# RWKV-7 mixer in a two-layer trunk: v without its head mean in the states, gate products on Vector, joins of the inverse cut into parts between products of v

## The chip, the cores and the metric

The kernel runs on one core of a Trainium2 chip. The metric is the device time of one execution in microseconds (us), median of several runs. TensorE's clock has two levels, 1.2 and 2.4 GHz; the profile gives the granted one as a share of the full clock.

## What is computed

A trunk of two layers over 256 tokens of width 1024: each layer is a feed-forward, a mixer, a feed-forward and a gated embedding, with RMS norms around each. The mixer of the first layer is a gMLP, that of the second an RWKV-7 mixer with 16 heads of 64, and only the latter is touched. Cut to what matters:

```python
r, k, v = ...                                 # three products of 1024x1024
g = sigmoid(xg @ g1) @ g2                     # gate, 1024 -> 160 -> 1024
y = wkv7_scan(r, decay, k, v, -kk, kk * a)    # state 64x64 per head:
#   S = S diag(w) + (S a) b^T + v k^T ;  y = S r     (i: value, j: key)
mean = mean(y, -1); var = mean((y - mean) ** 2, -1)      # over a head's 64 values
yn = (y - mean) * rsqrt(var + eps) * lnx[0] + lnx[1]
bonus = sum(r * k * r_k, -1) * v              # one factor for each token and head
out = ((yn + bonus) * g) @ w_out
```

Each row of the state belongs to one value dimension, and rows never mix. So the mean of y over a head's value dimensions is the y that the mean of v would give.

## The kernel before, in words

The program is one straight line of eight stages. Weights come in units of 128 rows: a load of 512 KB on SyncE's queue (`raw`, L134), a rounded high part by Scalar (L154) and the remaining low part by Vector (L156), three TensorE products for each pair. A table `on_pool` gives the low part of five of the eight units of the output weights `o` (`bwout`) to Pool. The weights of r, k, v and of the second gate product g2 are used in full precision and come as 1 MB loads (`wf`, L146) straight into a slot.

There are 20 slots of 128x2048 and 8 PSUM banks, both handed out in order from queues of free ones, so a load may start when the use of whatever held its slot has ended. A scheduler fixes the order on each engine from the order of the text; `behind(...)` ties work to come after a named instruction.

The mixer works in 4 chunks of 64 tokens (two blocks b of 128 tokens, two chunks in each). Its stages, with the names in the rows:

- The products r (L1174, in PSUM `r`) stand after the preparation of decay and keys, and are moved by the scheduler around two `triangle(i)` (L1033, `m`): products of keys whose triangles are to be inverted. Vector inverts diagonal blocks of 16 by forward substitution (L1069, L1071), between the transposes L1061 and L1072, L1073.
- Gate: `gate1` (L1129, four transposes L1140), `gate2` for both blocks (L1150, L1153), with the result `gn`.
- v: eight steps k of four products 128x512 (L1238). From step 2 on each step is followed by an `inside(k)` (L1218 `sc`, L1226 `rb`: products within a chunk, masked by Vector in L1221, L1228), and from step 4 on by a `join(i)`: the blocks of 16 are joined to 32 (`q` L1081, then `x` L1088) and to 64 (`q` L1098, then `x` L1112), each with a copy or an addition by Scalar or Vector behind it. One join is 128 or 64 small matrix products.
- `stack_v`: Scalar writes v into the states' stack `sv` (L1267, L1268, eight times 64x512). `tb` and the copies `bn` (L1308) turn keys. `bonus`: Pool multiplies v by the bonus factor and adds `lnx[1]` (L1293, L1294).
- `chunk(c)`, four times, one after the other through the state: `us` (L1337), `y` (L1357), `us` (L1363), copies to `sv` (L1365 Scalar, L1366 Vector), `st` (L1375) and the update (L1380, Vector), `y` (L1387). Then the norm of y: head mean and subtraction (L1399, L1400, L1402, `gs` and `yc`, Vector), square by Scalar (L1416), its sum `gv` (L1417 Vector, L1418 and L1419 Pool), the product `yo` (L1429 Vector).
- `gains(b, q)`, behind chunks 0 and 1: Pool multiplies v's share by the gate (L1167) and the gate by `lnx[0]` (L1168).
- `tail`: `yo` by the gate plus v's share (L1435, L1436), transposes (L275), then the output product `Dn` (L178 to L180, `o`).

## Time and profile before

| | |
|---|---|
| median of 3 runs | 1206.67 us (1204.51 to 1207.19) |
| the profiled execution, by the clock | 1207.52 us |
| its span in the profile | 1205.7 us, 18609 instructions |
| TensorE busy | 1160.7 us (96%) |
| Vector busy | 839.7 us (70%) |
| Scalar busy | 650.0 us (54%) |
| Pool busy | 98.3 us (8%), 109 instructions |
| DMA | 207.78 MB, mean 172 GB/s |
| instruction blocks loaded (queue q8) | 57, 0.93 MB |

The profile page cuts the span into 40 slices. TensorE is busy for nine tenths or more in nearly all of them; the dip, together with one of the granted clock, is in slices 27 to 32, about 785 to 960 us, the RWKV mixer. Times below are from the start of the span; a row `L1174 MATMUL r<-xr,wf` is an instruction of line 1174 that writes tile `r` from `xr` and `wf`, `x48` that 48 such stand together (a product of full precision, as all of r, v, gate and joins are, is counted twice there, and once in the orders of the next section), and the bracket behind it the idle time ahead of the first and what ended it. `issue` is a wait for nothing that the profile shows. Engines: PE is TensorE, PEld its weight load, DVE Vector, ACT Scalar, POOL GpSimd, SP SyncE.

### The profile page before, as it was taken

What the parts mean: (1) busy time and instruction counts of PE and PEld (TensorE: products, weight loads), DVE (VectorE), ACT (ScalarE), POOL (GpSimd) and SP (SyncE); (2) the same over time, 40 slices, a digit from 0 to 9 for tenths busy, and PEclk for the clock granted to TensorE, in tenths of its full rate; (3) what the DMA queues carried; (4) which work ended last, traced back from release to release, by engine and by line L of the source; (5) the groups of instructions that cost most, each with busy time, mean ns of one, the idle gap of its engine ahead of it and who ended that gap; (6) DMA issues with size and microseconds to landing.
All of it is one profiled execution on the core that took longest, in us unless ns stands there. A gap on an engine that the chain in (4) does not pass through costs nothing. (4 is left out here: it accounts for less than half of the span.)

```text
span 1205.7 us, 18609 instructions
## 1 busy us (share of the span) xinstructions
PE 1160.7 (96%) x7252; PEld 954.4 (79%) x7252; DVE 839.7 (70%) x1272; ACT 650.0 (54%) x1125; POOL 98.3 (8%) x109
## 2 busy tenths in 40 slices
PE   8999999999999999999999999989987799999997
PEld 6888888888888888888888887576566678888886
DVE  5887667686787676668767644698355888766663
ACT  6665556454576555568655532454053276555553
POOL 0000001010010000012000001300009420000011
PEclk8999999999999999999999999998998799999999
DMA  7886655656667666655666573113103267666510
GB/s 249 299 282 194 193 174 165 238 163 204 211 207 242 184 188 192 181 171 183 233 196 193 185 275 132 33 48 140 37 3 106 71 204 268 207 183 194 172 57 36
DMA packets 58778, 207.78 MB, mean 172 GB/s; under 512 B 6721, under 2 KB 7233, under 8 KB 58433
## 3 DMA queue, kind: packets, MB, share of 16 engines
q1 hardware_dynamic: 58688, 206.59, 52.6%
q8 instruction: 57, 0.93, 0.3%
q14 instruction: 33, 0.26, 0.1%
HBM read 205.51 MB, written 1.05 MB: 171 GB/s over the span
## 5 line engine op out<-in xcount | busy, mean ns | idle before, releaser
L156 DVE TENSOR_TENSOR w<-raw,w 128x1024 fp32r<-128x1024 f32 x335 | 408.0, 1224 | 142.3 <-ACT w L154 136.2
L154 ACT CAST w<-raw 128x1024 fp32r<-128x1024 f32 x340 | 357.5, 1056 | 154.3 <-PE mm L400 65.3
L400 PE MATMUL mm<-xT,w 128*128 128x512 f32 (+1 forms) x2304 | 407.8, 337 | 0.0
L400 PEld LDWEIGHTS mm<-xT,w 128*128 128x128 f32 x2304 | 358.5, 189 | 50.0
L178 PE MATMUL acc<-w,hT 128*128 128x512 f32 x352 | 138.2, 393 | 0.0
L179 PE MATMUL acc<-w,hT 128*128 128x512 f32 x352 | 137.3, 390 | 0.0
L180 PE MATMUL acc<-w,hT 128*128 128x512 f32 x352 | 137.1, 389 | 0.0
L408 ACT COPY pn<-mm 128x256 f32<-128x256 f32 x144 | 46.6, 375 | 99.2 <-PE mm L400 99.2
L409 DVE TENSOR_TENSOR pn<-mm,pn 128x256 f32<-128x256 f32 x144 | 54.3, 419 | 47.4 <-ACT pn L408 47.4
L180 PEld LDWEIGHTS acc<-w,hT 128*128 128x128 f32 x352 | 66.1, 188 | 14.2
L178 PEld LDWEIGHTS acc<-w,hT 128*128 128x128 f32 x352 | 66.2, 188 | 12.6
L179 PEld LDWEIGHTS acc<-w,hT 128*128 128x128 f32 x352 | 66.3, 188 | 12.3
L232 POOL TENSOR_SCALAR rpost<-ss 128x1 f32<-128x1 f32 x15 | 7.4, 494 | 770.8 <-ACT junk L239 770.8
L178 PE MATMUL mm<-w,xT 128*128 128x512 f32 x128 | 51.8, 414 | 3.7 <-ACT w L154 3.1
L179 PE MATMUL mm<-w,xT 128*128 128x512 f32 x128 | 51.7, 407 | 0.6 <-DVE xT L289 0.5
L289 DVE SCALAR_TENSOR_TENSOR xT<-tr,gT,xT 128x128 fp32r<-128x128 f32 x112 | 35.7, 344 | 23.5 <-ACT xT L288 22.7
L412 DVE TENSOR_TENSOR pn<-pn,yc 128x512 f32<-128x512 f32 x72 | 49.7, 690 | 2.1
L180 PE MATMUL mm<-w,xT 128*128 128x512 f32 x128 | 50.9, 403 | 0.0
L179 PE MATMUL z<-w,xT 128*128 128x512 f32 x128 | 49.9, 390 | 0.0
L180 PE MATMUL z<-w,xT 128*128 128x512 f32 x128 | 49.9, 390 | 0.0
L178 PE MATMUL z<-w,xT 128*128 128x512 f32 x128 | 49.7, 393 | 0.0
L288 ACT ACTIVATE xT<-tr,gT 128x128 fp32r<-128x128 f32 x112 | 37.9, 372 | 19.3 <-PE tr L275 15.2
(277 smaller groups left out, 1546.9 us busy)
## 6 DMA issues: line engine op xcount, KB each, us to landing
raw<-in_w SPq DMA_DIRECT2D x264, 512.0 KB, 4.2
raw<-in_win SPq DMA_DIRECT2D x32, 512.0 KB, 4.3
wf<-in_wrkv SPq DMA_DIRECT2D x12, 1024.0 KB, 5.2
raw<-in_wout SPq DMA_DIRECT2D x16, 512.0 KB, 4.7
raw<-in_wg SPq DMA_DIRECT2D x16, 512.0 KB, 4.0
gbc<-in_norm_g SPq DMA_DIRECT2D x9, 512.0 KB, 4.7
...
```

What stands on the lines that cost most here:

```text
L154: self.high = self.nc.scalar.copy(hh, r[:p, :n])
L156: eng.tensor_tensor(ll, r[:p, :n], hh.bitcast(F32), op=ALU.subtract)
L178: mm(out, lhsT=lh, rhs=rh, start=start, stop=False)
L179: mm(out, lhsT=ll, rhs=rh, start=False, stop=False)
L180: mm(out, lhsT=lh, rhs=rl, start=False, stop=stop)
L232: nc.gpsimd.tensor_scalar(r, a, b, eps, op0=ALU.add, op1=ALU.add)
L288: done = (nc.scalar.activation(hi, v, AF.Copy, scale=gc), nc.vector.scalar_tensor_tensor(lo, v, gc, hi.bitcast(F32), op0=ALU.mult, op1=ALU ...
L289: nc.vector.scalar_tensor_tensor(lo, v, gc, hi.bitcast(F32), op0=ALU.mult, op1=ALU.subtract))
L400: nc.tensor.matmul(ps[i][:, :T] if s else ps[i], lhsT=w[:, sl], rhs=x, start=u + q + s == 0, stop=s + u == 2 and q == 3)
L408: nc.scalar.copy(zi, ps[i][:, T:])
L409: nc.vector.tensor_tensor(zi, ps[i][:, :T], zi, op=ALU.add)
L412: nc.vector.tensor_tensor(z2, z2, rbc.unsqueeze(1).to_broadcast([128, 2, T]), op=ALU.mult)
```

## The change

1. The table for Pool goes; all low parts of `o` are Vector's (L156).
2. The r products (`r_step(k)`) stand in the text by the triangles: steps 0 to 3 ahead of the first, 4 to 6 ahead of the second, 7 behind.
3. v starts right behind `gate1`; `gate2` comes behind v, among the parts of join 3. The gate's transposes are apart (`gate_t`), behind the first step of v. The mixing products for v (L822) stand ahead of Vector's transpose L1072. The load of g2 is issued ahead of the first of v, into the slot of `hnT`; v's first goes to that of `dxT`.
4. Every join is cut into four parts, which stand between the four products of a step of v (joins 0 to 2 in steps 5, 6, 7) or with `gate2` (join 3). The insides come later: 0 and 1 behind step 5, 2 and 3 behind step 6, 4 to 7 behind step 7.
5. `vm`, the head mean of v, is taken once (Vector), and `stack_v` puts v less its mean into the states (Vector, one operation for each 64x512). The mean of y is zero then, so the three Vector operations on it in each chunk become one Scalar copy `yc`. The bonus still uses all of v.
6. `gains()`: Vector forms, ahead of the chunks, the gate times `lnx[0]` (`gx`), times `lnx[1]` (`lg`) and times the bonus factor; `vgain(b)` behind chunks 0 and 1 takes v by the last and adds `lg`. Pool's L1293, L1294, L1167, L1168 go. Both `lnx` rows are loaded early, ahead of the last r weights.

```diff
-        share = (("o", (0, 2, 5, 6, 7)),)
-        self.on_pool.update(at[n] + k for n, ks in share for k in ks)
...
+        def r_step(k):
+
+            w = self.need(at["r"] + k // 2)[0][:, k % 2]
+            for m in range(KT):
+                mm(psr[m // 2][:, (m % 2) * T:(m % 2 + 1) * T], lhsT=w[:, m * 128:(m + 1) * 128], rhs=xent(0, k),
+                   start=k == 0 and m % 2 == 0, stop=k == KT - 1 and m % 2 == 1)
+            if k % 2:
+                self.release(at["r"] + k // 2)
+
         for i in range(2):
             if i:
                 squares(i)
             decay(i)
             V.tensor_tensor(bt[:, hs(i)], kk[:, hs(i)], av[:, hs(i)], op=ALU.mult)
             ab(i)
+            for k in (range(4, 7) if i else range(4)):
+                r_step(k)
             triangle(i)
+        r_step(7)
         self.drop(eo)
+        self.drop(X["x"][0])
...
+        def pieces(n, do, last):
+
+            r = [lambda lo=lo: do(range(lo, lo + n // 4)) for lo in range(0, n, n // 4)]
+            return r[:3] + [lambda: (r[3](), last())]
+
         def join(i):
...
+                def do(ns):
+                    for n in ns:
+                        for o in range(0, 128, 32):
+                            mm(ps[o:o + 32, n * 16:(n + 1) * 16], lhsT=nx[o:o + 16, n, :], rhs=wv[o:o + 16, n, 0:16], start=True, stop=True)
+
+                def last():
+                    S.copy(qn[:, :, 0:16], ps.rearrange("p (n t) -> p n t", t=16))
+                    self.unbank(ps)
...
+            return pieces(32, do, last)
...
+        def gate_t():
+
+            gl, ps = G8["s"], G8["p"]
+            gn = gl[:, 1024:1536].rearrange("p (b n) -> p b n", b=2)
...
+            return [lambda: main(0), lambda: main(1), rest]
...
+        def gains():
 
             gn = X["gn"]
-            if b == 0 and q == 0:
-                G8["la"] = self.gain_tile(io["lnx"][0:1, :])
-            bs = slice(b * D + q * 512, b * D + (q + 1) * 512)
-            G.tensor_tensor(vn[:, bs], vn[:, bs], gn[:, bs], op=ALU.mult)
-            G.tensor_tensor(gn[:, bs], gn[:, bs], G8["la"][:, q * 512:(q + 1) * 512], op=ALU.mult)
-
-
-        for k in range(KT):
-            w = self.need(at["r"] + k // 2)[0][:, k % 2]
+            X["gx"], X["lg"] = self.slot("gx"), self.slot("lg")
+            la, lb = (self.gain_tile(io["lnx"][n:n + 1, :]) for n in range(2))
+            for b in range(NB):
+                bs = slice(b * D, (b + 1) * D)
+                V.tensor_tensor(X["gx"][:, bs], gn[:, bs], la, op=ALU.mult)
+                V.tensor_tensor(X["lg"][:, bs], gn[:, bs], lb, op=ALU.mult)
+                g3 = gn[:, bs].rearrange("p (h t) -> p h t", t=64)
+                V.tensor_tensor(g3, g3, bon[:, b * 16:(b + 1) * 16].unsqueeze(2).to_broadcast([128, 16, 64]), op=ALU.mult)
...
+        def vgain(b):
+
+            for q in range(2):
+                bs = slice(b * D + q * 512, b * D + (q + 1) * 512)
+                V.tensor_tensor(vn[:, bs], vn[:, bs], X["gn"][:, bs], op=ALU.mult)
+                V.tensor_tensor(vn[:, bs], vn[:, bs], X["lg"][:, bs], op=ALU.add)
...
-        X["gn"] = self.slot("gn")
-        for b in range(NB):
-            gate2(b)
...
+        def v_step(k, between=()):
+
             x = xent(2, k)
             w = self.need(at["v"] + k // 2)[0][:, k % 2]
+            between = list(between)
             for b in range(NB):
                 for q in range(2):
                     mm(psv[b][q], lhsT=x[:, b * 128:(b + 1) * 128], rhs=w[:, q * 512:(q + 1) * 512], start=k == 0, stop=k == KT - 1)
+                    if between:
+                        between.pop(0)()
             if k % 2:
                 self.release(at["v"] + k // 2)
-            if k in (1, 3):
-                P(1, 0)
-            if k > 1:
-                inside(k - 2)
-            if k > 3:
-                if k == 7:
-                    self.drop(X["x"][2])
-                    xx = self.slot("xx")
-                    xv = xx.rearrange("p (n t) -> p n t", t=64)
-                    for o in (32, 96):
-                        G.memset(xv[o:o + 32, :, 0:32], 0.0)
-                join(k - 4)
-        inside(6)
-        inside(7)
+
+        v_step(0)
+        gate_t()
+        v_step(1)
+        P(1, 0)
+        v_step(2)
+        v_step(3)
+        P(1, 0)
+        v_step(4)
+        xx = self.slot("xx")
+        xv = xx.rearrange("p (n t) -> p n t", t=64)
+        for o in (32, 96):
+            G.memset(xv[o:o + 32, :, 0:32], 0.0)
+        v_step(5, join(0))
+        inside(0)
+        inside(1)
+        v_step(6, join(1))
+        self.drop(nq)
+        bo_sums()
+        P(2, 4)
+        inside(2)
+        inside(3)
+        v_step(7, join(2))
+        self.drop(X["x"][2])
+        X["gn"] = self.slot("gn")
+        inside(4)
         vn = self.slot("vn")
         for b in range(NB):
             for q in range(2):
                 S.copy(vn[:, b * D + q * 512:b * D + (q + 1) * 512], psv[b][q])
         self.unbank(*psv[0], *psv[1])
+        inside(5)
+        j3 = join(3)
+        g2 = gate2(0)
+        for n in range(2):
+            g2[n]()
+            j3[2 * n]()
+            j3[2 * n + 1]()
+        g2[2]()
+        self.drop(wu_, mx)
+        inside(6)
+        for n in gate2(1):
+            n()
+        inside(7)
+        gains()
...
+        vm = self.small(32, "vm", 1)
+        vmv = vm.rearrange("p (b m h) -> p b m h", b=2, h=2)
+        for b in range(NB):
+            V.tensor_reduce(vm[:, b * 16:(b + 1) * 16], vn[:, b * D:(b + 1) * D].rearrange("p (h t) -> p h t", t=64), axis=AX.X, op=ALU.add)
+            V.tensor_scalar(vm[:, b * 16:(b + 1) * 16], vm[:, b * 16:(b + 1) * 16], ck[:, 0:1], 1.0 / 64, op0=ALU.mult, op1=ALU.mult)
 
         def stack_v(c):
             rs = half[c % 2]
-            S.activation(svv[c // 2][OD, c % 2, :, 0, :], vv[rs, c // 2, :, 0, :], AF.Copy, scale=ck[rs, 0:1])
-            S.activation(svv[c // 2][EV, c % 2, :, 1, :], vv[rs, c // 2, :, 1, :], AF.Copy, scale=ck[rs, 0:1])
+            for h in range(2):
+                V.scalar_tensor_tensor(svv[c // 2][half[1 - h], c % 2, :, h, :], vv[rs, c // 2, :, h, :], ck[rs, 0:1],
+                                       vmv[rs, c // 2, :, h].unsqueeze(2).to_broadcast([64, 8, 64]), op0=ALU.mult, op1=ALU.subtract)
...
-                    s = self.small(4, "gs", 4)
-                    V.tensor_reduce(s, yv_, axis=AX.X, op=ALU.add)
-                    V.tensor_scalar(s, s, 1.0 / 64, None, op0=ALU.mult)
                     yc = self.small(256, "yc", 4)
-                    L["n"] = V.tensor_tensor(r4(yc), yv_, s.unsqueeze(2).to_broadcast([128, 4, 64]), op=ALU.subtract)
+                    L["n"] = S.copy(yc, yp[:, :256])
...
-                e.tensor_tensor(yo[:, sl], yo[:, sl], X["gn"][:, sl], op=ALU.mult)
+                e.tensor_tensor(yo[:, sl], yo[:, sl], X["gx"][:, sl], op=ALU.mult)
...
         chunk(0)
-        with behind("n"):
+        with behind("c"):
             P(1, 0)
-            for q in range(2):
-                gains(0, q)
+            vgain(0)
         chunk(1)
-        with behind("n"):
+        with behind("c"):
             P(1, 0)
-            for q in range(2):
-                gains(1, q)
+            vgain(1)
+        self.drop(X["gn"], X["lg"])
```

What moves on the engines, at three places. First TensorE at join 0 (`q`, 32x16 products of the inverse) and the step of v around it; `rb` is the end of an inside. Before:

```order
L1226 MATMUL rb_7290<-sk_7197,bt_6873 64x64 x8
L1081 MATMUL q_596_7311<-wu_6759,nq_6996 32x16 x128
L1238 MATMUL v_7218<-wf_7263,xr_7177 128x512
L1238 MATMUL v_7219<-wf_7263,xr_7177 128x512
L1238 MATMUL v_7220<-wf_7263,xr_7177 128x512
L1238 MATMUL v_7221<-wf_7263,xr_7177 128x512
```

And now:

```order
L1296 MATMUL v_7194<-wf_7225,xr_7153 128x512
L1099 MATMUL q_584_7234<-wu_6759,nq_7062 32x16 x32
L1296 MATMUL v_7195<-wf_7225,xr_7153 128x512
L1099 MATMUL q_584_7234<-wu_6759,nq_7062 32x16 x32
L1296 MATMUL v_7196<-wf_7225,xr_7153 128x512
L1099 MATMUL q_584_7234<-wu_6759,nq_7062 32x16 x32
L1296 MATMUL v_7197<-wf_7225,xr_7153 128x512
L1099 MATMUL q_584_7234<-wu_6759,nq_7062 32x16 x32
```

The 128 products of the join (256 rows of the trace) stood in one piece between an inside and the next step of v; now 32 of them stand behind each of the four products of one step.

Then Vector just ahead of the copies `bn`, where `sk` and `rb` are the masked results of the last insides. Before:

```order
L1221 TENSOR_TENSOR sk_7199<-sc_7797,mk 64x512
L1221 TENSOR_TENSOR sk_7199<-sc_7798,mk 64x512
L1221 TENSOR_TENSOR sk_7199<-sc_7817,mk 64x512
L1221 TENSOR_TENSOR sk_7199<-sc_7818,mk 64x512
L1228 TENSOR_TENSOR rb_7217<-rb_7796,mk 128x512
L1308 COPY bn_7855<-tb_7857 64x256 x2
```

And now:

```order
L1276 TENSOR_TENSOR sk_7175<-sc_7850,mk 64x512
L1276 TENSOR_TENSOR sk_7175<-sc_7851,mk 64x512
L1283 TENSOR_TENSOR rb_7193<-rb_7821,mk 128x512
L1208 TENSOR_TENSOR gx_7871<-gn_7695,gbc 128x1024
L1209 TENSOR_TENSOR lg_7872<-gn_7695,gbc 128x1024
L1359 SCALAR_TENSOR_TENSOR sv_7884<-vn_7717,ck,vm 64x8x64
L1211 TENSOR_TENSOR gn_7695<-gn_7695,bon 128x1024
L1378 COPY bn_7900<-tb_7902 64x256 x2
```

The gain products (L1208, L1209, L1211: `gx`, `lg` and the gate times the bonus factor) and the states' v (L1359, `sv`) stand between the last masks and ahead of `bn`.

Last, Vector in the second chunk, from the norm of the chunk before to the update of the state and `yo`. Before:

```order
L1399 TENSOR_REDUCE gs<-y_7954 128x4
L1399 TENSOR_REDUCE gs<-y_7966 128x4
L1400 TENSOR_SCALAR gs<-gs 128x4 x2
L1402 TENSOR_TENSOR yc<-y_7954,gs 128x256
L1402 TENSOR_TENSOR yc<-y_7966,gs 128x256
L156 TENSOR_TENSOR w_8526<-raw,w_8526 128x1024
L1417 TENSOR_REDUCE gv<-k_8105 128x4
L1417 TENSOR_REDUCE gv<-k_8108 128x4
L1366 COPY sv_7843<-us_8080 64x4x64
L1366 COPY sv_7843<-us_8092 64x4x64
L1380 TENSOR_TENSOR sv_7844<-st_8113,gC 64x4x64 x2
L1380 TENSOR_TENSOR sv_7844<-st_8130,gC 64x4x64 x2
```

And now:

```order
L1448 TENSOR_TENSOR sv_7883<-st_8010,gC 64x4x64 x2
L156 TENSOR_TENSOR w_8079<-raw,w_8079 128x1024
L1233 TENSOR_TENSOR vn_7717<-vn_7717,gn_7695 128x512 x2
L1234 TENSOR_TENSOR vn_7717<-vn_7717,lg_7872 128x512 x2
L1482 TENSOR_REDUCE gv<-k_8113 128x4
L1482 TENSOR_REDUCE gv<-k_8116 128x4
L1434 COPY sv_7883<-us_8088 64x4x64
L1434 COPY sv_7883<-us_8100 64x4x64
L1448 TENSOR_TENSOR sv_7884<-st_8121,gC 64x4x64 x2
L1448 TENSOR_TENSOR sv_7884<-st_8138,gC 64x4x64 x2
L1494 TENSOR_TENSOR yo_7974<-yc,gv 64x4x64 x4
```

The six operations on the mean are gone; a split and four products on v (`vn`) stand ahead of the copy of `us` that the state needs.

## Rows read from the trace of the kernel before

**Rows 1.** Stretches: us; busy (instructions) of PE, PEld, DVE, ACT, POOL; PEclk, DMA share, GB/s.

```profile
877.10:906.37 29.27, 27.08 (x509) 19.23 (x510) 19.25 (x34) 19.24 (x35) 0.00 (x0) 0.95 0.01 3
925.83:945.17 19.34, 10.99 (x194) 9.79 (x192) 10.55 (x21) 3.04 (x7) 12.36 (x11) 0.68 0.45 137
985.00:1150.00 165.00, 164.36 (x866) 140.59 (x866) 121.02 (x175) 98.35 (x162) 1.99 (x2) 1.00 0.66 209
```

**Rows 2.** What TensorE waited for, 783 to 985 us: total, times, longest.

```profile
PE st L1375 <- ACT sv L1365: 10.7, 2, 8.3
```

**Rows 3.** The chain of work that ended last: start, length, what.

```profile
926.38 4.91 POOL gn L1168 x4
...
931.68 1.67 POOL gv L1419
...
939.48 0.27 ACT sv L1365
```

**Rows 4.** TensorE's timeline up to v: start, length, instructions, [idle before <- releaser].

```profile
786.37 10.63 PE L1174 MATMUL r<-xr,wf 128*128 128x256 f32 x48
799.33 2.08 PE L1033 MATMUL m<-kk,bt 64*64 64x64 f32 x64 [2.33 <-DVE bt L1004]
...
814.28 2.81 PE L1033 MATMUL m<-kk,bt 64*64 64x64 f32 x64 [2.32 <-DVE wu L1059]
...
824.89 4.51 PE L1129 MATMUL g<-wf,xr 128*128 128x160 f32 x32
...
832.76 3.51 PE L1150 MATMUL g<-wf,gl 128*128 128x512 f32 x4 [1.20 <-ACT gl L1141]
...
840.22 10.57 PE L1238 MATMUL v<-wf,xr 128*128 128x512 f32 x24
```

**Rows 5.** TensorE's timeline, v and the joins q and x.

```profile
851.83 3.70 PE L1238 MATMUL v<-wf,xr 128*128 128x512 f32 x8
...
861.32 2.03 PE L1081 MATMUL q<-wu,nq 16*32 16x16 f32 x221
865.70 0.49 PE L1081 MATMUL q<-wu,nq 16*32 16x16 f32 x35 [2.36 <-issue]
...
876.24 0.88 PE L1088 MATMUL x<-mx,nq 32*32 32x16 f32 x75 [1.99 <-issue]
```

**Rows 6.** DMA queues in 862 to 864.5 us: packets, MB, share of 16 engines.

```profile
q8 instruction: 1, 0.02, 3.4%
```

**Rows 7.** DMA issues in 812 to 822 us: count, KB each, us to landing.

```profile
wf<-in_g SPq DMA_DIRECT2D x1, 1024.0 KB, 7.2
```

**Rows 8.** Vector's groups by shape, 765 to 985 us: busy us, mean ns, idle before.

```profile
L156 DVE TENSOR_TENSOR w<-raw,w 128x1024 fp32r<-128x1024 f32 x11 | 13.6, 1263 | 0.4 <-ACT w L154 0.2
L822 DVE SCALAR_TENSOR_TENSOR xr<-dxT,chT,hnT 128x256 f32<-128x256 f32 x26 | 11.8, 475 | 0.0
L1221 DVE TENSOR_TENSOR sk<-sc,mk 64x512 f32<-64x512 f32 x16 | 11.0, 689 | 30.1 <-PE sc L1218 16.0 <-PE rb L1226 13.8
...
L894 DVE TENSOR_REDUCE gn<-junk 128x8 f32<-128x512 f32 x4 | 2.7, 677 | 0.8 <-ACT junk L893 0.8
...
L1048 DVE TENSOR_TENSOR bt<-kk,a 128x1024 f32<-128x1024 f32 x2 | 2.4, 1206 | 0.0
```

**Rows 9.** Vector's timeline, a transpose of the inverse and the chunks.

```profile
819.34 1.96 DVE L1061 STREAM_TRANSPOSE wu<-mx 128x1024 f32<-128x1024 f32 x1 [2.81 <-ACT mx L1040]
...
912.16 0.88 DVE L1380 TENSOR_TENSOR sv<-st,gC 64x256 f32<-64x256 f32 x2 [0.42 <-PE st L1375]
...
933.38 3.85 DVE L1429 TENSOR_TENSOR yo<-yc,gv 64x256 f32<-64x256 f32 x4 [8.26 <-POOL gv L1419]
...
957.25 1.71 DVE L1429 TENSOR_TENSOR yo<-yc,gv 64x256 f32<-64x256 f32 x4
```

**Rows 10.** TensorE's timeline, the last chunk and the first transpose of the output.

```profile
945.17 1.15 PE L1337 MATMUL us<-sv,sk 128*64 128x64 f32 x32
...
952.15 1.09 PE L275 MATMUL tr<-ident,yo 128*128 128x128 f32 x4 [1.97 <-DVE yo L1436]
```

More of the change, by code (lines that the diff above doesn't have):

```diff
@@ L1090, in join, with do @@
-                self.unbank(ps)
-                V.transpose(wu_[:, 1024:], md)
+                        c0 = o // 32 % 2 * 32
+                        (V.tensor_copy if c0 else S.copy)(xv[o:o + 32, :, c0:c0 + 32], xt[o:o + 32])
             elif i == 2:
-                for hh in range(2):
-                    ps = self.bank("q2")
-                    for i in range(16):
-                        n = hh * 16 + i
+                ps = [self.bank("q2") for _ in range(2)]
+                def do(ns):
+                    for n in ns:
@@ new lines, in rest @@
+            def rest():
+                for q in range(2):
+                    r = slice(32 * (2 * b + q), 32 * (2 * b + q) + 32)
+                    mm(pg[q], lhsT=gl[r, T + b * 128:T + (b + 1) * 128], rhs=w[r, 1, sl[q]], start=False, stop=True)
+                for q in range(2):
+                    S.copy(gn[:, b * D + q * 512:b * D + (q + 1) * 512], pg[q])
+                self.unbank(*pg)
+                if b:
+                    self.release(at["g2"])
+                    self.drop(gl)
@@ new lines, in bo_sums @@
+        def bo_sums():
+            rkb, sel = hsel[:, :256].rearrange("p (m h) -> p m h", h=32), hsel[:, 256:]
+            G.tensor_tensor(rkb, rkb, vec(4).unsqueeze(2).to_broadcast([128, 8, 32]), op=ALU.mult)
+            ps = self.bank("bo")
+            for m in range(KT):
+                o = m % 4 * 32
+                mm(ps[o:o + 32, :T], lhsT=rkb[:, m], rhs=g8(kT)[:, m], start=m < 4, stop=m >= 4)
+            bo = self.small(256, "k1", 6)
+            S.copy(bo, ps[:, :T])
+            for b in range(NB):
+                mm(ps[:, T + b * 16:T + (b + 1) * 16], lhsT=bo[:, b * 128:(b + 1) * 128], rhs=sel, start=b == 0, stop=b == 1)
+            S.copy(bon, ps[:, T:T + 32])
+            self.unbank(ps)
+            self.drop(kT)
```

97 lines of the change are left out of this document (30 added, 67 removed).

## The prediction

> **What bounds the kernel now.** I read the table of stretches first, to see where TensorE is not the bound. In 985 to 1150 us it is busy for 164.36 of 165.00 us, in 925.83 to 945.17 us for 10.99 of 19.34 [rows 1]: after the RWKV mixer time only passes through. How much earlier the mixer's output product can start is the whole question; what follows it keeps its order and its length. TensorE's waits name the largest hole, two waits of a state product for a copy of Scalar, 10.7 us together, one of them 8.3 [rows 2]. The chain shows that Scalar is not its cause: the copy `sv` comes behind Pool's gain products L1168 (4.91 us) and then the `gv` that the normalization needs, both on Pool's one queue [rows 3]. The timelines tell the rest: two waits of 2.3 us in front of the triangles [rows 4], two holes with no releaser but the engine's own issue inside the joins [rows 5], and Vector held for 8.26 us by that `gv` [rows 9].
>
> All durations are of one profiled execution (span 1205.7 us, 1207.52 by the clock), 0.85 above the median of the runs, 1206.67. A measurement of this kernel can tell about 0.2%, 2.4 us.
>
> **Term 1, up to the end of the x products.** Before, they end at 877.1, where the first stretch of [rows 1] begins.
> The r products are cut 64, 48, 16 in place of 48, 48, 32 (the trace counts a product of full precision twice). At 10.63 us for 48 [rows 4], 64 take 14.2 and end at 800.5; the first triangle, let go by Vector at 799.33, waits no more. With 2.1 for it and 10.6 for the next 48, TensorE is at 813.3; the second is let go at 814.28 as before, a wait of 1.0. Then 2.8, 3.5 for the last 16 and 4.5 for the gate: 825.
> v's first load needs the slot of `dxT`, so the end of v's mixing products L822. All eight now stand ahead of the transpose that waited 2.81 us for Scalar until 819.34 [rows 9]: 8 x 0.475 [rows 8] from 816.5 is 820. There the loads of g2 and of v go out, 1 MB each and g2's first. Beside another such load one took 7.2 us [rows 7], so v starts at 827.5. Before, it started at 840.22: the second gate product (832.76 to 840.22, 7.5 us) [rows 4] now comes behind v.
> From 827.5: six steps of v at 10.57/3 = 3.52 (21.1), four gate transposes 1.1, q products 2.03 + 0.49, two insides of 1.1 each (the gap from 840.22 + 10.57 to 851.83), the seventh step 3.52, x products 2.6 like q's [rows 4, 5, 10]. That is 860.5.
> The parts add switches. A step of v, eight in the trace, takes 3.70 between two insides against 3.52, 0.18 a switch; eight make 1.4.
> The holes of 2.36 and 1.99 us lie inside rows of 256 tiny products, after 221 and 181 of them [rows 5]. At 863.1 a block of TensorE's instructions moves [rows 6]. I read the hole as products used up faster than their instructions come. With a v product of 0.88 (3.52/4) ahead of each quarter of them it should shrink, not vanish: between 0 and 4.35 us I take 1.4, nearer nothing, since 181 to 221 products passed without a hole, and a part has 64. So x ends at **863.4, 13.7 earlier**. The Trainium skill (Runtime: NRT & Kernel Launch, section Instruction fetch mechanics) says that the sequencer streams blocks of 256 instructions by itself and that crossing one is mostly hidden. By that rule the holes have another cause and the parts need not help; the trace speaks against it with the block that moves inside the hole.
>
> **Term 2, from there to the first state.** Vector becomes the chain. Before, it was busy for 19.25 of 29.27 us, 877.10 to 906.37 [rows 1]. Added:
> - two head sums 128x16 from 128x1024. No row has them: a 128x512 reduction took 0.677 [rows 8], so between 0.7 and 1.4; I take 1.25, nearer twice the row. With two tiny scalings 2.8.
> - eight 64x512 products of `stack_v`, until now Scalar's: L1221 of this shape took 0.689; 5.5.
> - six 128x1024 gain products at L1048's 1.206: 7.3.
> - masks of insides 2 and 3, which stood ahead of x's end: four at 0.689 and one alike, 3.4.
>
> Sum 38.2 with no idle time left. TensorE's own work there, 27.08 less a v step, plus 7.5 of gate and two insides, is below 34 and not the bound. The copies `bn` end at 901.6 in place of 906.37. Before, a split and a wait, 2.5 together, stood between them and the first state, complete at 913.04 [rows 9]; now it needs two copies, half a us of state product and the update, 3.1, and is there at 904.7: **lead 8.3**. More than a third of the first lead is eaten. That Scalar loses eight products saves nothing here; it is not on the chain.
>
> **Term 3, the chunks.** Before, from 913.04 to the first transpose of the output at 952.15 [rows 10]: 39.1. After:
> - Chunk 1 goes by TensorE. Its work in the stretch of a chunk was 10.99 us at a granted clock of 0.68 in the mean [rows 1], 7.5 at the full one; with two handoffs 8.2. Vector beside it (split 1.26, four `vgain` of 0.68, sums, copies and update of 0.4 to 0.44 each) has 7.4, just hidden.
> - Chunk 2 goes by Vector: four `yo` 1.71 [rows 9], split 1.26, `vgain` 2.7, two sums and two copies 1.6, a split 1.26, half a us for the state product, update 1.76: 10.8.
> - To the transpose: 945.17 to 952.15 less its wait of 1.97 is 5.0 [rows 10]; with handoffs 6.3.
>
> Sum 25.3, **gain 13.8**. The subtraction of the mean (L1399, L1400, L1402) leaves Vector for Scalar copies. Of the five splits that come from Pool, three are counted above, two lie beside the output product, which lasts longer than both.
> Costed at nothing: the two `lnx` loads go out long before and nothing is late behind them; the bonus sums lie under Vector's chain on TensorE; the output's weights are loaded and split no later. Without that cover each would cost its own time.
>
> Lead 8.3 + 13.8 = 22.1. Four handoffs not counted, at 0.4 like the 0.42 in front of an update [rows 9], take back 1.6. 1207.52 - 22.1 + 1.6 = 1187.0, less 0.85 to stand against the median: **1186**. Own range 1182 to 1192: holes 0 to 4.35, sums 0.7 to 1.4, handoffs 0 to 4.
>
> **Rivals.**
> (a) *Vector becomes slow* (slower). Four `yo` products took 3.85 us at 933.38, beside Pool's work, and 1.71 at 957.25 [rows 9], 2.25 times. If Vector's new work runs at such a rate, 26.9 us (15.6 and 3.4 in front, 7.9 of splits and `vgain`) gain 33.6: 1186 + 34 = 1220. It decides from a factor of 1.76, where 26.9 x 0.76 = 20.5 is the whole gain. For it: those rows. Against: Pool's large products are just what goes; it keeps memsets and scalings of 128x8. 0.05.
> (b) *The lead up to x is lost*: v lands late behind g2, or every part meets its own hole. Then 1186 + 13.7 = 1200. For it: v's landing rests on one row. Against: each part is followed by a v product as cover. 0.15.
> (c) *The chunks gain half*: copies, splits and `vgain` on one Vector queue make each chunk wait for the one before; 7 less, 1193. For it: chunk 2 is already Vector's. Against: the waits for `gv` go in any case. 0.2.
> (d) *The holes are no matter of instruction blocks*, and the parts give nothing of 4.35 back: 3 more, 1189. For it: no releaser is named. Against: [rows 6]. The page above would have it so. 0.1.
> (e) *More than this*: TensorE's clock stays up where it was 0.68 in the mean, between its levels of 1.2 and 2.4 GHz [rows 1], in the output product too, no hole is left and chunk 2 hides its splits: 6 more, 1180. Against: Vector's chain leaves TensorE idle before the chunks as well. 0.1.
> (f) *The change doesn't do what it says*: a `gv` is still late, behind something else, and the 8.3 us stay: 1194. Against: nothing large is left in front of it on Pool. 0.03.
>
> **How the numbers follow.** Forecast 0.37, (c) 0.2, (b) 0.15, (d) 0.1, (e) 0.1, (a) 0.05, (f) 0.03. The range, 1178 to 1200, leaves out (a) and the far sides of (b) and (e). Faster 0.93; the same 0.02, (b) with slow handoffs; slower 0.05.
>
> **What would show it.** A wait near 1 us before the second triangle and none before the first; v from about 827.5 after a wait for a DMA; x ending near 863; Vector without idle time from there to `bn`; first state near 905; chunk periods of 8 and 11 us without a `gv` wait; the first transpose of the output near 930; 985 to 1150 us as full as before, 20 us earlier. It is wrong if Vector's new rows are longer than 0.69 and 1.21, if holes of 2 us appear within the parts, or if the output product waits for its weights.

## The result and the profile after

Before 1205.59 us (median of 4 runs), changed 1187.85 us (4 runs, 1186.54 to 1189.20): ratio 0.985, interval 0.9833 to 0.9866, some 18 us faster. The forecast was 1186 us, 1178 to 1200, with a chance of 0.93 for faster. The profiled execution has a span of 1185.8 us against 1205.7, 19.9 less; 20.5 had been worked out.

The stretches after, cut at the same events (x products ended; first state complete; second; third; first transpose of the output), with the columns of [rows 1]:

```profile
865.63:910.57 44.94, 37.32 (x689) 26.86 (x690) 40.73 (x63) 19.02 (x40) 1.05 (x2) 0.92 0.08 26
910.57:918.14 7.57, 7.57 (x204) 6.83 (x204) 6.84 (x14) 3.77 (x10) 1.99 (x2) 1.00 0.23 71
918.14:928.06 9.92, 8.78 (x216) 7.78 (x212) 9.65 (x18) 5.58 (x12) 1.98 (x2) 1.00 0.25 76
928.06:931.90 3.84, 2.83 (x74) 2.48 (x72) 3.72 (x8) 3.41 (x8) 0.00 (x0) 1.00 0.23 89
965.00:1130.00 165.00, 165.00 (x868) 140.81 (x867) 121.78 (x175) 98.52 (x162) 2.08 (x3) 1.00 0.67 210
```

Chunks of 12.1 and 19.2 us (913.04 over 925.13 to 944.34 before) became 7.57 and 9.92; the granted clock in them is 1.00 where it was 0.84 and 0.68 (the latter in [rows 1]). Pool is busy for 2 us of a chunk, Vector for nearly all of it. Behind the mixer TensorE is as full as before.

TensorE's timeline up to the end of x and at the first transpose of the output, for [rows 4, 5, 10]:

```profile
785.87 14.08 PE L1046 MATMUL r<-xr,wf 128*128 128x256 f32 x64
799.88 2.08 PE L1030 MATMUL m<-kk,bt 64*64 64x64 f32 x64
...
813.78 2.08 PE L1030 MATMUL m<-kk,bt 64*64 64x64 f32 x64 [1.26 <-DVE wu L1070]
...
827.80 6.68 PE L1296 MATMUL v<-wf,xr 128*128 128x512 f32 x8 [3.94 <-DMA wf<-in_wrkv]
...
834.75 14.76 PE L1296 MATMUL v<-wf,xr 128*128 128x512 f32 x34
...
865.43 0.20 PE L1110 MATMUL x<-mx,nq 32*32 32x16 f32 x2 [0.32 <-issue]
...
931.90 0.41 PE L275 MATMUL tr<-ident,yo 128*128 128x128 f32 x2 [0.79 <-DVE yo L1501]
932.24 1.14 PE L1455 MATMUL y<-sv,rb 64*64 64x64 f32 x30
```

The first triangle waits no more, the second 1.26 us; v starts at 827.80. Two things are not as in the sum: v's wait for its load is 3.94 us long (2.5 there), and its first step behind that takes 6.68 us where a step takes 3.52. Of the two holes in q and x only 0.32 is left. The first transpose `tr` stands ahead of most of the last chunk's products `y`.

Vector's timeline from there, for [rows 9]:

```profile
865.67 0.69 DVE L1113 TENSOR_TENSOR mx<-x,mx 128x512 f32<-128x512 f32 x1 [5.87 <-PE x L1110]
...
899.72 7.08 DVE L1378 COPY bn<-tb 64x256 f32<-64x256 f32 x16
...
908.78 1.79 DVE L1448 TENSOR_TENSOR sv<-st,gC 64x256 f32<-64x256 f32 x4
...
918.17 1.72 DVE L1494 TENSOR_TENSOR yo<-yc,gv 64x256 f32<-64x256 f32 x4
```

The copies `bn` begin 34 us behind x, the first state is complete at 910.57, and `yo` takes 1.72 us for four, with no wait for a `gv`.

### The profile page after: what moved, and what is told of

Read it like the earlier page. It is cut to its first block, busy times and chain, and to the rows that moved or that the text cites. A ratio compares the mean times of both kernels' runs of the same rounds, so it can differ in the third digit from the quotient of the medians.

```text
span 1185.8 us, 18581 instructions
## 1 busy us (share of the span) xinstructions
PE 1151.6 (97%) x7252; PEld 945.9 (80%) x7252; DVE 850.0 (72%) x1279; ACT 647.2 (55%) x1125; POOL 69.7 (6%) x92
## 4 chain that ended last, share of the span: by engine, by line
PE 83%; DVE 9%; DMA 3%; ACT 2%; issue 1%; POOL 1%; SPq 0%; POOLq 0%; DVEq 0%; ACTq 0%
PE mm L400 34%; PE acc L178 7%; PE acc L179 7%; PE acc L180 7%; PE v L1296 3%; PE z L178 2%; PE z L180 2%; PE z L179 2%; PE k L877 2%; DMA raw<-in_w 2%; PE mm L179 2%; PE mm L180 2%; PE mm L178 2%; DVE w L156 2%; PE tr L275 1%
## 5 line engine op out<-in xcount | busy, mean ns | idle before, releaser
L156 DVE TENSOR_TENSOR w<-raw,w 128x1024 fp32r<-128x1024 f32 x340 | 413.7, 1223 | 143.5 <-ACT w L154 137.6
L288 ACT ACTIVATE xT<-tr,gT 128x128 fp32r<-128x128 f32 x112 | 37.9, 372 | 18.1 <-PE tr L275 13.6
```

Source lines behind the costliest of these rows:

```text
L156: eng.tensor_tensor(ll, r[:p, :n], hh.bitcast(F32), op=ALU.subtract)
L288: done = (nc.scalar.activation(hi, v, AF.Copy, scale=gc), nc.vector.scalar_tensor_tensor(lo, v, gc, hi.bitcast(F32), op0=ALU.mult, op1=ALU ...
```

## Experiments

Twelve kernels, each with one edit to the changed kernel (e1 to e6, e9, e11, and three together in e12) or to the kernel before (e7, e8, e10). This table is worked out from the timelines of TensorE and Vector as differences between the same events, so that the shift of a whole run of about a microsecond drops out: from the first r product to the first of v; to the last of x; to the first state; two chunks; to the first transpose of the output; and the sum of these. Ratios are to the kernel before on the same chip.

| kernel | to v | to x | to first state | two chunks | to output | sum | ratio (95%) |
|---|---|---|---|---|---|---|---|
| before | 53.9 | 36.9 | 35.9 | 31.3 | 7.8 | 165.8 | 1 |
| changed | 41.9 | 37.8 | 44.9 | 17.5 | 3.8 | 146.0 | 0.9850 (0.9833 to 0.9866) |
| e1 joins whole | 42.0 | 39.8 | 45.6 | 17.5 | 3.8 | 148.8 | 0.9869 (0.9841 to 0.9896) |
| e2 r behind triangles | 41.2 | 34.4 | 44.9 | 17.5 | 3.9 | 141.9 | 0.9798 (0.9766 to 0.9830) |
| e3 gate product ahead of v | 37.8 | 40.7 | 41.8 | 17.5 | 3.8 | 141.7 | 0.9810 (0.9782 to 0.9838) |
| e4 mean in the chunks | 42.2 | 36.0 | 45.1 | 21.1 | 5.3 | 149.6 | 0.9907 (0.9878 to 0.9935) |
| e5 bn mostly by Scalar | 42.4 | 37.1 | 41.5 | 18.7 | 3.8 | 143.5 | 0.9827 (0.9809 to 0.9845) |
| e6 front gains on Pool | 42.1 | 37.7 | 41.4 | 17.5 | 3.9 | 142.5 | 0.9823 (0.9806 to 0.9839) |
| e9 g2's load behind v's | 38.7 | 34.9 | 45.0 | 17.5 | 3.9 | 139.8 | 0.9792 (0.9771 to 0.9813) |
| e11 splits on Pool | 42.0 | 36.0 | 46.9 | 18.6 | 8.0 | 151.4 | 0.9889 (0.9868 to 0.9911) |
| e12 = e2 + e5 + e6 | 41.2 | 34.5 | 41.5 | 19.0 | 3.8 | 140.0 | 0.9785 (0.9763 to 0.9807) |
| e7 before, gains on Vector | 52.4 | 36.7 | 43.2 | 22.2 | 8.5 | 163.0 | 0.9977 (0.9962 to 0.9992) |
| e8 before, mean-free v | 52.5 | 36.5 | 40.7 | 26.1 | 10.0 | 165.7 | 1.0019 (1.0009 to 1.0028) |
| e10 before, gains and splits on Vector | 55.3 | 37.9 | 39.9 | 21.5 | 4.5 | 159.0 | 0.9922 (0.9898 to 0.9946) |

How far these figures carry: the stages of a row come from one profiled execution. The changed kernel, e4, e5, e6 and e11 are alike up to the end of x, and yet take 36.0 to 37.8 us from v to x, so a difference below 2 us there means nothing by itself. The medians named below come from several chips; where they and the ratios differ, the ratios decide. By these, e1 and e5 cannot be told from the changed kernel, and e6 only just.

**e1, the joins whole again.**

```diff
-        v_step(5, join(0))
+        v_step(5)
+        for n in join(0):
+            n()
...
```

> The changed kernel, but joins 0, 1 and 2 whole behind their step of v, not in four parts. Theory (instruction blocks): the holes inside the q and x rows come back, about 2 us each where 0.3 was left, the eight switches of 0.18 go; x ends 2 to 4 us later than 865.6, and since Vector's chain begins there, the whole is 2 to 4 us slower (about 1191). Rival (the cutting does nothing for the holes, or Vector's chain has slack): no hole, same time or 1 us faster.

TensorE's waits (us in total, times, longest) in e1:

```profile
PE q L1099 <- issue: 2.1, 1, 2.1
PE x L1110 <- issue: 2.1, 1, 2.1
```

Both holes are back, 2.1 us each, and x comes later in spite of a first step of v that is 1.3 us shorter here (5.37); the sum is 2.8 us more. The holes belong to long rows of tiny products: the cut is what removed them. That it was worth the 2.8 us is not shown by the ratios (0.9869 and 0.9850, with overlapping intervals). That the cause is the loading of instruction blocks is not shown either: a block moves just ahead of each hole in e1 too (at 851 and at 864 us), but in 835 to 885 us eight blocks move in the changed kernel, where the holes are gone, and seven in e1.

**e2, r behind both triangles; e9, the load of g2 behind those of v.**

```diff
-            for k in (range(4, 7) if i else range(4)):
-                r_step(k)
             triangle(i)
-        r_step(7)
...
+        for k in range(KT):
+            r_step(k)
         rT = self.slot("rT")
```

> The changed kernel, but the r products in one loop behind both triangles in the text, as before. Theory: TensorE waits again about 2.3 us twice in place of 1.3 once and reaches the gate 3.4 us later, but v starts at 827.8 by its load, for which TensorE waits 3.9 us now; so v starts within 0.5 us of 827.8 and the whole is the same (1187 to 1189). Rival (the r placement gave its 3.4 us to the end): 1191.

It was neither: 4.1 us less in the sum, ratio 0.9798 (median 1183.08). TensorE waits 2.33 and 2.24 us at the triangles again and reaches v 0.7 us earlier by the table, but does not stand still there. TensorE's timeline in e2:

```profile
826.79 3.60 PE L1295 MATMUL v<-wf,xr 128*128 128x512 f32 x8
```

The first step takes 3.60 us where it takes 6.68 in the changed kernel. SyncE's queue issued v's first load at 819.56 there and at 814.75 here, because Vector's mixing products for v came earlier among its other work. The last of them, on Vector's timeline, first in the changed kernel and then in e2:

```profile
816.28 2.85 DVE L819 SCALAR_TENSOR_TENSOR xr<-dxT,chT,hnT 128x256 f32<-128x256 f32 x7
```

```profile
812.28 2.06 DVE L819 SCALAR_TENSOR_TENSOR xr<-dxT,chT,hnT 128x256 f32<-128x256 f32 x5
```

Two causes then, the wait itself and the slow step behind it; e9 leaves the r products alone and only turns the two loads round:

```diff
-        put("g2", [(io["g2"], 128, D, 2)])
         put("v", rows(2))
+        put("g2", [(io["g2"], 128, D, 2)])
```

> The changed kernel, but g2's load is issued behind v's loads, not ahead of the first. Theory (the r placement cost time in e2 because TensorE stood still for v's load and its clock fell behind that): v starts without a wait, its first step takes 3.5 us and not 6.7; x ends 4 to 5 us earlier, held from there by Vector's inverse, and the whole is 4 to 5 us faster, 1183. Rival (what e2 gained came from Vector's order, not from the load): 1 us at most.

The wait and the step behind it, by stretches of the changed kernel, with the columns of [rows 1] (the granted clock is the third number from the end):

```profile
824.00:826.00 2.00, 0.00 (x0) 0.00 (x0) 1.94 (x5) 1.95 (x6) 0.00 (x0) 1.00 0.91 369
826.00:827.80 1.80, 0.00 (x1) 0.03 (x1) 1.77 (x3) 0.09 (x1) 1.55 (x2) 0.79 0.04 16
827.80:830.00 2.20, 2.20 (x3) 1.14 (x4) 2.17 (x5) 0.00 (x0) 0.34 (x1) 0.50 0.00 0
827.00:835.00 8.00, 7.20 (x13) 3.29 (x14) 7.52 (x18) 0.04 (x1) 1.08 (x2) 0.57 0.49 162
```

And in e9 the stretch 827 to 835 us, then its first step of v on TensorE's timeline:

```profile
827.00:835.00 8.00, 8.00 (x23) 3.81 (x22) 7.51 (x18) 1.63 (x2) 1.89 (x2) 1.00 0.68 254
```

```profile
823.95 3.67 PE L1296 MATMUL v<-wf,xr 128*128 128x512 f32 x8 [0.65 <-DVE sk L1257]
```

In the changed kernel the granted clock is 1.00 for the first 2 us of the standstill, falls in the rest of it, and is 0.50, the lower of its two levels (1.2 GHz), when the products of v begin. In e9 the row puts the 0.65 us ahead of v down to Vector's `sk`; but v's first load, issued at 818.61, lands after 5.2 us, at 823.8, so it is still the load that v waits for. Behind g2's load, in the changed kernel, it takes 8.1 us. The clock is at 1.00 where the mean of the same stretch was 0.57, and the first step takes 3.67: 6.2 us less in the sum, median 1181.41, more than the 4 to 5 expected. So the changed kernel gives away about 6 us where it lets g2's megabyte go first: 3.3 in the wait (3.94 less 0.65) and 3.0 in the slow step (6.68 less 3.67), less what the inverse would have taken in any case (q waits 0.5 for it in e9). The 3.0 is of one execution: behind stops of 3.9 to 4.4 us the same step took 5.37 in e1, e4 and e11, 6.06 in e5 and 6.52 in e6. In e1 the clock was still 1.00 at the end of the stop and 0.57 in the first 2.2 us of the step.

**e3, the second gate product ahead of v.** Its two blocks stand between the first gate product and v, and the fourth join is then in one piece:

```diff
-        v_step(0)
+        X["gn"] = self.slot("gn")
         gate_t()
+        for b in range(NB):
+            for n in gate2(b):
+                n()
+        v_step(0)
...
-        g2 = gate2(0)
-        for n in range(2):
-            g2[n]()
-            j3[2 * n]()
-            j3[2 * n + 1]()
-        g2[2]()
+        for n in j3:
+            n()
...
-        for n in gate2(1):
-            n()
```

> The changed kernel, but the second gate product of both blocks stands ahead of v again (7.5 us of TensorE). Theory: x ends 5 to 7.5 us later than 865.6; Vector's chain starts that much later and has nothing to hide it, so the whole is 5 to 7 us slower (about 1194). Rival (TensorE's 7.5 us behind x count as much as ahead of it): same within 2 us.

The expectation fell: 4.4 us less, but not by the place of the product. v's first load was issued ahead of g2's (812.03 and 818.67 us), so TensorE had v and then the gate to work on and no hole. The place of the product shows against e9, which has no such hole either: up to the end of x e3 takes 4.9 us more, and from there to the first state 3.2 less. So of TensorE's 7.5 us a good part counts on either side of x. The stretch behind x is therefore not Vector's alone; TensorE and Vector take turns.

**e4, the mean of y in the chunks, v with its mean in the states.**

```diff
-        vm = self.small(32, "vm", 1)
...
-                V.scalar_tensor_tensor(svv[...], vv[...], ck[rs, 0:1], vmv[...], op0=ALU.mult, op1=ALU.subtract)
+            S.activation(svv[...], vv[...], AF.Copy, scale=ck[rs, 0:1])
...
+                    V.tensor_reduce(s, yv_, axis=AX.X, op=ALU.add)
+                    V.tensor_scalar(s, s, 1.0 / 64, None, op0=ALU.mult)
...
-                    L["n"] = S.copy(yc, yp[:, :256])
+                    L["n"] = V.tensor_tensor(r4(yc), yv_, s..., op=ALU.subtract)
```

> The changed kernel, but v with its mean in the states again: stack_v by Scalar, and the mean of y taken off in each chunk by Vector (two sums, two scalings, two subtractions, 1.8 us). Theory (Vector is the chain from x to the output): 8.9 us of Vector leave the front, some 5 of them up to the end of bn since TensorE's tb then binds, and 1.8 come to each of two to three chunks; within 3 us of the change, so this part is not where the gain is from. Rival (the mean was what held the chunks): 5 us or more slower, 1193 and up.

The rival's number holds: 1195.92, 8.1 more than the change (6.9 by the ratios). The chunks grow by 3.6 and the way to the output by 1.5, as costed; but the 8.9 us that leave Vector in front give nothing there (45.1 against 44.9). Vector's timeline in e4:

```profile
875.66 0.68 DVE L1131 COPY wu<-q 32x512 f32<-32x512 f32 x1 [2.68 <-PE q L1125]
...
885.93 1.22 DVE L1208 TENSOR_TENSOR gx<-gn,gbc 128x1024 f32<-128x1024 f32 x1 [2.15 <-ACT gn L1194]
...
905.50 0.43 DVE L1427 COPY sv<-us 64x256 f32<-64x256 f32 x1 [0.68 <-ACT sv L1426]
```

It waits for TensorE's join and for the gate instead, and behind `bn` for Scalar, which now has `stack_v` and bn. The other 3.4 us lie behind the first transpose of the output (28.1 us to the next transposes, of `h`, on TensorE; 24.7 in the changed kernel). There the subtraction stands between Vector's splits; that this costs the 3.4 is argued, not shown.

**e5, bn by bank: six of eight banks by Scalar.**

```diff
-                    (S.copy if h else V.tensor_copy)(bnv[...], pv[half[c], :, h, :])
+                    (S.copy if (b * 2 + i) * 2 + g < 6 else V.tensor_copy)(bnv[...], pv[half[c], :, h, :])
```

> The changed kernel, but the copies bn are cut by PSUM bank and not by half: six of the eight banks all by Scalar, two by Vector (8 copies of Vector in place of 16). Theory (Vector is the chain up to the first state, Scalar has idle time there): bn ends 3 to 3.5 us earlier, and the whole is 3 us faster, about 1185. Rival (TensorE or Scalar binds there): same, within 1 us.

The first state comes 3.4 us earlier, as expected; the next chunk gives 1.2 back. Median 1184.95. TensorE's timeline in e5 has a new wait ahead of the first state, for Scalar's copies `k`, which stand behind its 24 copies `bn`:

```profile
901.77 1.55 PE L1431 MATMUL us<-k,xx 64*64 64x64 f32 x32 [2.75 <-ACT k L1407]
```

**e6, the six front gain products on Pool.**

```diff
-                V.tensor_tensor(X["gx"][:, bs], gn[:, bs], la, op=ALU.mult)
-                V.tensor_tensor(X["lg"][:, bs], gn[:, bs], lb, op=ALU.mult)
+                G.tensor_tensor(X["gx"][:, bs], gn[:, bs], la, op=ALU.mult)
+                G.tensor_tensor(X["lg"][:, bs], gn[:, bs], lb, op=ALU.mult)
...
-                V.tensor_tensor(g3, g3, bon..., op=ALU.mult)
+                G.tensor_tensor(g3, g3, bon..., op=ALU.mult)
```

> The changed kernel, but the six gain products ahead of the chunks on Pool (vgain stays on Vector). Pool is empty there, so no gv is queued behind anything. Theory (Vector loses time beside large Pool operations, as one yo of 2.55 us against 0.42 did): Vector saves 7.3 us but its operations beside the 14 us of Pool stretch; same or slower, 1187 to 1193. Rival (only Pool's queue was bad, the engines do not hurt each other): 4 to 7 us faster, 1181 to 1184.

3.5 us less, between the two: median 1183.86. The timelines of e6, Vector's and then Pool's:

```profile
890.58 4.06 DVE L1359 SCALAR_TENSOR_TENSOR sv<-vn,ck,vm 64x512 f32<-64x512 f32 x2
894.68 1.41 DVE L1276 TENSOR_TENSOR sk<-sc,mk 64x512 f32<-64x512 f32 x2
...
896.61 7.06 DVE L1378 COPY bn<-tb 64x256 f32<-64x256 f32 x16
```

```profile
891.28 2.82 POOL L1209 TENSOR_TENSOR lg<-gn,gbc 128x1024 f32<-128x1024 f32 x1
```

Two L1359, which read two tensors from SBUF, take 4.06 us beside Pool where two take 1.50 alone; the masks L1276 and the copies `bn`, which read from PSUM, take what they always do (1.41 and 7.06). So it matters what Vector does while Pool works. The Trainium skill (SBUF — State Buffer, section SBUF: two separate sides) says that the two engines share a pair of ports under an exclusive lock, which a Vector operation with two inputs from SBUF needs as well; these rows agree, 2.6 us lost by two operations beside the end of one Pool product and the whole of the next, 2.82.

**e7, e10 and e11: who does Pool's work.** e7 moves only the gain and bonus products of the kernel before to Vector; e10 is e7 and moves the five splits as well; e11 gives the splits of the changed kernel back to Pool.

```diff
-            G.tensor_tensor(vn[:, bs], vn[:, bs], gn[:, bs], op=ALU.mult)
-            G.tensor_tensor(gn[:, bs], gn[:, bs], G8["la"][:, q * 512:(q + 1) * 512], op=ALU.mult)
+            V.tensor_tensor(vn[:, bs], vn[:, bs], gn[:, bs], op=ALU.mult)
+            V.tensor_tensor(gn[:, bs], gn[:, bs], G8["la"][:, q * 512:(q + 1) * 512], op=ALU.mult)
...
-                G.tensor_tensor(hv4, hv4, bon..., op=ALU.mult)
-                G.tensor_tensor(vn[:, bs], vn[:, bs], lb, op=ALU.add)
+                V.tensor_tensor(hv4, hv4, bon..., op=ALU.mult)
+                V.tensor_tensor(vn[:, bs], vn[:, bs], lb, op=ALU.add)
```

The two lines that e10 takes out and e11 puts back:

```diff
-        share = (("o", (0, 2, 5, 6, 7)),)
-        self.on_pool.update(at[n] + k for n, ks in share for k in ks)
```

> The kernel before, with nothing changed but that bonus and gain products (L1293, L1294, L1167, L1168) run on Vector. Theory (gv behind Pool's gain products is the main loss of the chunks): the waits of 8.3 and the stretched L1400 and L1429 go, 10.3 us of Vector come; the whole is 5 to 13 us faster, about 1197. Rival (Vector has no room for them, only the mean-free v makes it): same or slower, 1205 and up.

> The kernel before, with the gain and bonus products and also the five splits on Vector; Pool keeps only the tiny operations. Theory (it is Pool's large operations beside Vector that stretch Vector's, in e7 still the splits): L1429 takes 1.7 for four again and not 3.7, L1400 0.2 and not 2.2; 6 to 8 us less than e7 there, 3.7 more for three splits on the path: 1199 to 1201. Rival (the splits on Pool are cover): 1205 and up.

> The changed kernel, but the five splits of the output weights are Pool's again. Theory (same): two of three splits leave Vector's path, 2.5 us, and Vector operations beside Pool's 2.4 us stretch by about as much: within 2 us of 1188, rather slower. Rival (a queue on Pool costs nothing as long as gv is not behind it): 3 us faster.

e7 gave 2 us, between the theory's 5 to 13 and the rival's nothing; e10 gave 9 (1196.44; its profiled execution, 1199.70, is the slowest of the four, so the table shows less), more than I had expected; in e11 the change loses 5.5 us (1193.35; 4.7 by the ratios), also more. Five timelines follow, in this order: Vector's and Pool's in e7, Vector's in e10, Vector's and Pool's in e11.

```profile
908.90 4.51 DVE L1294 TENSOR_TENSOR vn<-vn,gbc 128x1024 f32<-128x1024 f32 x2
...
927.61 3.71 DVE L1429 TENSOR_TENSOR yo<-yc,gv 64x256 f32<-64x256 f32 x4
...
945.39 2.16 DVE L1400 TENSOR_SCALAR gs<-gs 128x4 f32<-128x4 f32 x1
```

```profile
909.99 5.63 POOL L156 TENSOR_TENSOR w<-raw,w 128x1024 fp32r<-128x1024 f32 x2 [63.00 <-ACT w L154]
...
927.38 2.36 POOL L156 TENSOR_TENSOR w<-raw,w 128x1024 fp32r<-128x1024 f32 x1 [0.64 <-ACT w L154]
...
945.18 2.34 POOL L156 TENSOR_TENSOR w<-raw,w 128x1024 fp32r<-128x1024 f32 x1 [1.76 <-ACT w L154]
```

```profile
910.00 2.35 DVE L1292 TENSOR_TENSOR vn<-vn,gbc 128x1024 f32<-128x1024 f32 x2
...
926.10 1.72 DVE L1427 TENSOR_TENSOR yo<-yc,gv 64x256 f32<-64x256 f32 x4
```

```profile
896.44 2.72 DVE L1361 SCALAR_TENSOR_TENSOR sv<-vn,ck,vm 64x512 f32<-64x512 f32 x1
...
918.75 3.70 DVE L1496 TENSOR_TENSOR yo<-yc,gv 64x256 f32<-64x256 f32 x4
...
929.74 3.82 DVE L1496 TENSOR_TENSOR yo<-yc,gv 64x256 f32<-64x256 f32 x4
933.59 3.32 DVE L1502 TENSOR_TENSOR yo<-yo,gx 128x512 f32<-128x512 f32 x2
```

```profile
894.77 3.84 POOL L156 TENSOR_TENSOR w<-raw,w 128x1024 fp32r<-128x1024 f32 x1 [18.54 <-issue]
...
918.52 2.36 POOL L156 TENSOR_TENSOR w<-raw,w 128x1024 fp32r<-128x1024 f32 x1 [0.87 <-ACT w L154]
...
929.96 2.43 POOL L156 TENSOR_TENSOR w<-raw,w 128x1024 fp32r<-128x1024 f32 x1 [1.10 <-ACT w L154]
933.25 2.51 POOL L156 TENSOR_TENSOR w<-raw,w 128x1024 fp32r<-128x1024 f32 x1 [0.86 <-ACT w L154]
```

Without the waits for `gv` the two chunks of e7 are 9.1 us shorter, but its first state comes 7.2 us later behind x: the bonus products now stand on Vector ahead of it. And every split on Pool stretches the operation of Vector that it meets: L1294 4.51 in place of 2.35, L1429 3.71 and 3.79 in place of 1.72. L1400, a scaling of 4 columns with one tensor as its input, takes 2.16 in place of 0.17, so two inputs are not needed for it. Four of the five splits in e11 do the same on the way to the output (2.72 for one L1361 of 0.75; 3.70, 3.82; 3.32 for L1502, 1.29 alone); the fifth stands beside v, off that way. Not every operation in reach pays: L1211 of e11, with two inputs and wholly within the 3.84 us of the first of these splits, took its usual 1.21. A split that costs Vector 1.22 us costs it about 2 us when Pool does it. So in the changed kernel the removal of one line, the share of Pool, is worth 5.5 us, more than the 2 that the gain products give alone in the kernel before.

**e8, the kernel before with mean-free v only** (the reverse of e4, in the kernel before).

```diff
+        vm = self.small(32, "vm", 1)
...
-            S.activation(svv[c // 2][OD, c % 2, :, 0, :], vv[rs, c // 2, :, 0, :], AF.Copy, scale=ck[rs, 0:1])
...
+                V.scalar_tensor_tensor(svv[...], vv[...], ck[rs, 0:1], vmv[...], op0=ALU.mult, op1=ALU.subtract)
...
-                    V.tensor_reduce(s, yv_, axis=AX.X, op=ALU.add)
...
-                    L["n"] = V.tensor_tensor(r4(yc), yv_, s..., op=ALU.subtract)
+                    L["n"] = S.copy(yc, yp[:, :256])
```

> The kernel before, with nothing changed but v less its head mean in the states, by Vector. Theory: the chunks still wait for gv behind Pool; Vector gains 8 us of work in a stretch where it is idle for 10, and loses 1.8 in each chunk: 0 to 4 us faster, 1202 to 1206. Rival (the mean operations are what makes the chunks long): 8 us or more faster, below 1198.

2 us slower, outside both ends. Its chunks still stand for Pool. Vector's timeline in e8, then Pool's:

```profile
896.36 4.58 DVE L1274 SCALAR_TENSOR_TENSOR sv<-vn,ck,vm 64x512 f32<-64x512 f32 x6
...
930.30 4.85 DVE L1433 TENSOR_TENSOR yo<-yc,gv 64x256 f32<-64x256 f32 x4 [7.15 <-POOL gv L1423]
...
941.09 7.91 DVE L1433 TENSOR_TENSOR yo<-yc,gv 64x256 f32<-64x256 f32 x4
```

```profile
941.30 7.42 POOL L156 TENSOR_TENSOR w<-raw,w 128x1024 fp32r<-128x1024 f32 x3 [2.07 <-ACT w L154]
```

From x to the end of `bn` Vector has 8.6 us more work (27.85 us busy, 19.25 before), and only 4.2 of it falls into its idle time: six of the eight L1274 come in one piece behind the last mask, ahead of `bn`. So the first state is 4.8 us later. The two chunks are 5.2 shorter, though they still wait 7.15 for `gv`. On the way to the output 2.2 are lost again, where `yo` takes 7.91 us beside three splits of Pool in a row (3.80 before). The same edit that is worth 7 to 8 us in the changed kernel (e4) is worth nothing here.

**e12, three together:** the diffs of e2, e5 and e6 in one kernel.

> e2, e5 and e6 together: r products behind the triangles, six of eight banks of bn by Scalar, the six gain products ahead of the chunks on Pool. Theory: 4.7 from v's start, 2.3 to 3.4 from bn, 2 to 3.6 from the gains, less where TensorE's own tb binds then: 1175 to 1179. Rival (the three take the same time): 1182.

1181.03, ratio 0.9785 (0.9763 to 0.9807): faster than the change, no faster than e9 alone, and nearer the rival's 1182 than the theory. Of 3.5 and 2.5 from e6 and e5, 1.9 are left beyond e2. The timelines of e12, TensorE's and then Scalar's:

```profile
896.91 1.15 PE L1430 MATMUL us<-k,xx 64*64 64x64 f32 x32 [2.75 <-ACT k L1406]
...
900.00 1.97 PE L1442 MATMUL st<-sv,bn 128*64 128x64 f32 x28
```

```profile
887.36 9.10 ACT L1377 COPY bn<-tb 64x256 f32<-64x256 f32 x24
896.49 0.65 ACT L1406 COPY k<-us 128x256 f32<-128x256 f32 x2
```

The 24 copies of bn now stand on Scalar's queue ahead of the copies `k` that the first chunk needs: TensorE waits 2.75 us for them, as in e5, and its state products behind that take 1.97 us where 1.15 is usual, at a granted clock of 0.50 (900 to 904 us). Vector was no longer the limit there; Scalar's order was. e9 with a smaller share of bn for Scalar was not run.

## Why the prediction was right, and where not

The total was within 2 us by way of three terms that were off by 2.2, 3.6 and 4.0 us and 1.6 us of handoffs that did not come. That these cancelled, to 20.25 us at the first transpose for 20.5 forecast, is luck; that the mixer would give some 20 us, most of it in the chunks, is not.

- *Term 1, to the end of x: 13.7 earlier forecast, 11.5 measured* (865.63 against 877.12). The start of v (827.5 forecast, 827.80) and the waits at the triangles (1.0; 1.26) came out. The term failed at "six steps of v at 10.57/3": the first took 6.68 because TensorE had stood still ahead of it, a wait that the sum itself contained (825 to 827.5). [rows 4] had a sign of it: behind waits of 2.3 us the first triangle took 2.08 and the second 2.81, at a granted clock of 0.69 (814.28 to 817.10 us). The sum took the 2.8 for the product's own length; in the changed kernel it is 2.08. The holes were mis-sized the other way, 0.32 and not 1.4 (e1: 2.1 each without the cut). By the rule of the Trainium skill (Runtime: NRT & Kernel Launch, section Instruction fetch mechanics) that such crossings are mostly hidden the cut need not have helped; it did (4.2 us of holes in e1, 0.3 with the cut), and no run shows whether the holes are such crossings.
- *Term 2, to the first state: 41.3 from x forecast, 44.9 measured.* "Sum 38.2 with no idle time left": Vector was busy 38.2 of the 41.2 us up to the end of bn, exactly as summed, but idle for 3.0 between: 1.9 in waits for TensorE (a join, products that the masks read, the last product of v), the rest in gaps too small to have a name; behind bn it took 3.8 and not 3.1. The experiments show two engines: 7.5 us taken from TensorE make this stretch 3.1 shorter (e3), 7.3 taken from Vector 3.5 (e6), and 8.9 taken from Vector and given in part to Scalar nothing (e4). My chain had one. The lead at the first state was 2.5 and not 8.3.
- *Term 3, the chunks: 25.3 forecast, 21.3 measured.* 7.57 for 8.2, 9.92 for 10.8, 3.84 for 6.3. The last was the one mis-sized: the transposes do not wait for the last chunk, they stand among its products.
- *The wait for `gv` was the right hole, but half of the cause.* The prediction laid the gain to the queue in front of `gv`. e7 takes that queue away: the chunks give 9.1 us, of which Vector's new work in front takes 7.2 back, and 2 are left. With the splits off Pool too (e10) it is 9, and with the splits alone back (e11) 5.5 of the gain go. The other half is that Pool's operations stretch Vector's. I had these rows, 3.85 against 1.71 for `yo`, and used them for rival (a) alone, as a danger of the change, not as something that it removes. The same timeline of before has more: two scalings L1400 of 128x4 values took 4.34 us at 913.85, beside Pool, and 0.24 at 938.04.
- *Rivals.* (a), slower Vector, did not come: L1359 took 0.744 and the gain products 1.21. (b) is what took 2.2 us of the lead, by a cause that it did not name (the clock behind the wait). Of (d), that the parts give nothing back is refuted by e1, whose holes return; that the holes are no matter of instruction blocks stays open. Of (e) the clock came, 1.00 in the chunks, but no 6 us beyond the forecast. (c) and (f) did not come.
- *Not in the prediction:* that the r placement and the order of the loads work against each other. In this kernel the former is worth 4 us less than nothing (e2) and the latter costs 6 (e9). Whether the r placement pays once v's load goes first was not run.

What stays open: the clock's share of e9's 6 us, 3.0 by its rows, is known to about 1 us only, since the slow step took 5.37 to 6.68 in kernels that are alike up to there, and no kernel has the wait without it; what makes the holes in rows of tiny products; and the 3.4 us of e4 behind the first transpose.
